# A two-layer hybrid decoder trunk: one product of the first MLP matrix takes an earlier place among seven, and the transfers that build weight sums leave the mixer's last stages

## The chip, the cores and the metric

The kernel runs on one core of one Trainium2 chip. The metric is device time of one execution in microseconds (us), as the median of the runs; smaller is better. The engines are PE (TensorE, matrix products), DVE (VectorE), ACT (ScalarE), POOL (GpSimd) and SP (SyncE, which here only issues transfers). ACT and POOL issue transfers as well, each on a DMA queue of its own.

## The reference

Two layers, each a mixer and an MLP, on 512 tokens of width 1024, all in float32. The mixer's sliding-window attention and its mLSTM are as long as the rest together in code; what the change touches is the end of the mixer and the MLP.

```python
def hybrid_layer(x, ...):
    h = rmsnorm(x, norm_mix)
    z = h @ w_in                      # q,k,v | q,k,v,o of the mLSTM | its gates | branch gates
    ...
    att = sliding_window_attention(q_a, k_a, v_a, att_sinks)
    hm = mlstm_chunkwise(q_m, k_m, v_m, i_pre, f_pre)
    ...
    mixed = sigmoid(g_a) * (att @ w_att_branch) + sigmoid(g_m) * (hm @ w_m_branch)
    x = x + mixed @ w_out
    u = relu(rmsnorm(x, norm_ffn) @ w_ff1)
    return x + (u * u) @ w_ff2        # w_ff1: 1024 x 4096, w_ff2: 4096 x 1024
```

## The kernel before

**Precision.** Every weight and activation is split into a high part `wh` (ACT, a copy that rounds to fp32r) and a low part `wl` (DVE, the difference), and each product is three matmuls, high by high, high by low and low by high (`mm3`). So each weight tile passes through a DMA issued by SP, one ACT instruction and one DVE instruction before PE can use it. In the mixer that is a chunk of 128 x 512 (`chunk`, L192 and L193); in the MLP a block of 128 x 1024 (`w_split`, L915 and L916).

**The mixer** runs one long list of PE work (`weave`, L866) in which a chunk's twelve matmuls have width 1.0: queries, keys and values of attention; then mLSTM queries and keys, branch gates 0 and 1, mLSTM values, the attention branch (`a_steps`, two halves), gate 2, the output gate, gate 3. Attention, mLSTM and head work hang between these as side entries that have a place on the same scale. After it stand the mLSTM branch (the loop with `ev_m`, two halves `g` of the model width, `w_m_branch`) and the output projection (the loop with `ev_x`, `w_out`). `ev_m` takes a finished product out of PSUM with two DVE instructions (L873, L874) and splits it.

**The MLP** runs in four parts. Nearly every 2 x 2 block product is done with seven products and not eight: the plain blocks (0,0), (1,1), (1,0) of a weight matrix are products 1, 3 and 2, and sums of blocks, named A, B, D and C, are products 5, 6, 7 and 4. A is (0,0) + (0,1), D is (0,1) + (1,1), B is (0,0) + D, C is (1,0) + B. `first(part, i, u)` gives the seven products of the first matrix (`w_ff1`) for half `i` of a part, one `Slot` each; a slot is 24 matmuls of 128 x 256. `second(part, u)` gives the seven of the second matrix (`w_ff2`), 48 matmuls of 128 x 512 each in two runs. The slots of `second` of a part and of `first` of the next part are dealt into one list: after each slot of `second` come 2, 2, 2, 2, 3, 3 and 0 slots of `first`, taken in the order of the list that `first` returns.

**PSUM of the first matrix.** Products 1, 6 and 7 add up in bank `a`, 5 and 3 in bank `b`; `a` and `b` are the halves of one two-bank tile `mm`. Products 2 and 4 have a bank of their own, `c` and `d`, from a pool of two called `aux`. Between products of `mm` intermediate values are taken out: `copy` (L1109, ACT) after products 1, 5, 6 and 7, `finish` (L1113 on DVE, then two ACT instructions) after 3, 7, 2 and 4. All of them were recorded before the next product's matmuls, so the next product in `mm` waits for them.

**Weight sums.** A, B, C and D of both matrices are made in DRAM by transfers alone. `plan_sums` puts 79 jobs in a list, in the order in which they are needed: a copy of one half of a block (`Sums.copy`, issued by ACT behind the last weight split, L400, 512 KB), or an add of another onto it (`Sums.add`: POOL copies two numbers of the last weight split into `mark`, L403, and so waits for that split, then issues an accumulating transfer, L405, 512 KB). Each `beat` takes the next job. `beats(...)` places them: 26 in the mixer's long list, at every 2.5 from 2.5 to 40 and then every 2.0 from 42 to 60, 2 in the mLSTM branch, 8 in the output projection, 4 in the MLP's opening, and one after every second run of a slot.

**Order.** The code's order is where work is recorded; a list scheduler in the framework then orders each engine's instructions from it, from priorities (weight loads, splits and evacuations are high) and from its own estimate of durations. On each engine the queue is then fixed and runs in order.

## Time and profile before

| what | value |
|---|---|
| median of 3 runs (lowest to highest) | 1337.94 us (1337.82 to 1338.47) |
| the profiled execution: its own time | 1338.42 us |
| the profiled execution: span from first to last instruction | 1336.7 us |
| DVE, ACT, POOL busy | 72%, 57%, 17% of the span |
| DMA, mean | 177 GB/s |

The page's table of 40 slices shows where the DMA engines are full (each digit is a share in tenths of 33.4 us):

```profile
DMA  5545555689347988975326355565991589889843
```

A layer is half of the row. The 5s and 4s at its start are the mixer; the rise at the ninth and tenth digit is the mLSTM branch, the output projection and the MLP's opening; then come the four MLP parts, thinning out as the sums run out.

A row of the timeline has start, length, engine, line, operation, tile written and tiles read, shape, count, and in brackets the idle time before it with what ended it. A row of waits has the sum of idle time, how many waits, the longest. A row of windows has, for a stretch, each engine's busy time with its count, then the granted clock of PE, the busy share of the DMA engines and GB/s.

### The profile page before, as it was taken

Reading aid. Unit: us, or ns where it says so; the run is one execution under the profiler, and the core shown is the slowest. Engines: PE = TensorE matmul, PEld = TensorE weight load, DVE = VectorE, ACT = ScalarE, POOL = GpSimd, SP = SyncE. Lnnn points to the kernel's source line nnn. Section 1 sums busy time; section 2 is a strip of 40 time slices with the busy share of each in tenths; the row PEclk is TensorE's granted clock in tenths of the full one; section 3 lists DMA queues with packets and bytes.
Section 4 is the critical chain, followed back from the end, with each engine's and each line's share of the span. In section 5 each row is a group of like instructions: output and inputs, shape, how many; then the busy total and the mean of one; then the engine's idle time right before and its main releaser. Section 6 shows DMA issues by size and latency. Waiting matters only on the chain. (4 is left out here: it accounts for less than half of the span.)

```text
span 1336.7 us, 19393 instructions
## 1 busy us (share of the span) xinstructions
PE 1299.9 (97%) x6966; PEld 1101.6 (82%) x6966; DVE 957.3 (72%) x1493; ACT 763.1 (57%) x1367; POOL 225.3 (17%) x371
## 2 busy tenths in 40 slices
PE   8999999989999999999999999999899999999998
PEld 6877788878889889899878777888788898898986
DVE  4689764476568797978847887645746678979786
ACT  5468765544356555666544787554534565555663
POOL 4422410013001200220014134100110011002100
PEclk9999999999999999999999999999999999999999
DMA  5545555689347988975326355565991589889843
GB/s 150 155 128 126 108 135 157 199 237 217 98 140 217 281 214 280 220 208 173 103 80 182 110 136 110 137 191 166 242 247 50 156 228 274 230 258 223 228 153 126
DMA packets 154176, 236.36 MB, mean 177 GB/s; under 512 B 11608, under 2 KB 67008, under 8 KB 154080
## 3 DMA queue, kind: packets, MB, share of 16 engines
q1 hardware_dynamic: 111776, 154.76, 37.1%
q0 software_dynamic: 21056, 39.98, 17.8%
q10 hardware_dynamic: 21248, 40.38, 9.6%
q8 instruction: 55, 0.90, 0.3%
q14 instruction: 41, 0.34, 0.1%
HBM read 232.99 MB, written 81.79 MB: 235 GB/s over the span
## 5 line engine op out<-in xcount | busy, mean ns | idle before, releaser
L47 PE MATMUL mm<-i,wh 128*128 128x512 f32 (+1 forms) x1280 | 353.8, 362 | 1.6 <-ACT kvi L463 1.6
L916 DVE TENSOR_TENSOR wl<-raw,wh 128x1024 fp32r<-128x1024 f32 x212 | 257.1, 1220 | 73.4 <-ACT wh L915 73.1
L915 ACT ACTIVATE wh<-raw 128x1024 fp32r<-128x1024 f32 x212 | 222.4, 1053 | 151.6 <-PE mm L47 109.3
L47 PEld LDWEIGHTS mm<-i,wh 128*128 128x128 f32 x1280 | 224.9, 189 | 34.4 <-ACT kvi L463 2.4
L193 DVE TENSOR_TENSOR wl<-w,wh 128x512 fp32r<-128x512 f32 (+1 forms) x208 | 143.2, 690 | 133.3 <-ACT wh L192 132.3
L47 PE MATMUL mm<-i,wl 128*128 128x512 f32 (+1 forms) x640 | 229.7, 359 | 0.0
L192 ACT ACTIVATE wh<-w 128x512 fp32r<-128x512 f32 (+1 forms) x208 | 127.0, 612 | 163.0 <-PE mm L47 119.5
L403 POOL COPY mark<-wh 1x2 f32<-1x2 f32 x76 | 64.0, 843 | 713.0 <-ACT wh L915 481.4
L47 PE MATMUL mm<-wl,uh 128*128 128x512 f32 x448 | 175.0, 391 | 0.0
L47 PE MATMUL mm<-wh,uh 128*128 128x512 f32 x448 | 175.0, 391 | 0.0
L47 PE MATMUL mm<-wh,ul 128*128 128x512 f32 x448 | 174.6, 390 | 0.0
L47 PE MATMUL mm<-wh,i 128*128 128x512 f32 (+1 forms) x512 | 150.6, 371 | 0.4 <-ACT wh L192 0.4
L47 PEld LDWEIGHTS mm<-i,wl 128*128 128x128 f32 x640 | 120.9, 189 | 17.7
L47 PE MATMUL mm<-hs,wh 128*128 128x256 f32 x576 | 107.4, 287 | 5.5 <-ACT u L1109 5.5
L47 PEld LDWEIGHTS mm<-wh,i 128*128 128x128 f32 x512 | 92.3, 189 | 15.9 <-ACT wh L192 0.8
L47 PEld LDWEIGHTS mm<-hs,wh 128*128 128x128 f32 x576 | 90.0, 191 | 15.5 <-ACT u L1109 14.6
L47 PEld LDWEIGHTS mm<-wh,ul 128*128 128x128 f32 x448 | 84.2, 188 | 16.8
L47 PEld LDWEIGHTS mm<-wh,uh 128*128 128x128 f32 x448 | 84.3, 188 | 16.3
L47 PEld LDWEIGHTS mm<-wl,uh 128*128 128x128 f32 x448 | 84.3, 188 | 16.2 <-DVE wl L916 0.3
L47 PE MATMUL mm<-wl,i 128*128 128x512 f32 (+1 forms) x256 | 94.3, 368 | 0.0
L957 DVE SCALAR_TENSOR_TENSOR x<-mm,ninv,x 128x512 f32<-128x512 f32 x112 | 79.8, 745 | 16.2 <-PE mm L47 15.6
L47 PE MATMUL mm<-wh,a 128*128 128x512 f32 x256 | 82.9, 398 | 5.2 <-DVE a L873 5.2
(243 smaller groups left out, 2140.3 us busy)
## 6 DMA issues: line engine op xcount, KB each, us to landing
raw<-in_w_ff_dram SPq DMA_DIRECT2D x112, 512.0 KB, 6.0
sum<-in_w_ff_dram ACTq DMA_DIRECT2D x76, 512.0 KB, 4.6
raw<-sum SPq DMA_DIRECT2D x76, 512.0 KB, 5.2
w<-in_w_in_dram SPq DMA_DIRECT2D x128, 256.0 KB, 3.0
sum<-in_w_ff_dram POOLq DMA_DIRECT2D x44, 512.0 KB, 8.2
sum<-sum POOLq DMA_DIRECT2D x32, 512.0 KB, 7.5
w<-in_w_out_dram SPq DMA_DIRECT2D x32, 256.0 KB, 5.7
w<-in_w_att_branch_dram SPq DMA_DIRECT2D x16, 256.0 KB, 2.9
```

What stands on the lines that cost most here:

```text
L47: return nc.tensor.matmul(*args, **kw)
L192: last_wh[:] = sc.activation(wh[:, :off], raw[:, :off], AF.Copy), wh
L193: ve.tensor_tensor(wl[:, :off], raw[:, :off], f32(wh[:, :off]), op=ALU.subtract)
L403: m = gp.tensor_copy(mark, f32(last_wh[1][0:1, 0:2]))
L915: last_wh[:] = sc.activation(hi, r, AF.Copy), hi[:, 0, :]
L916: ve.tensor_tensor(lo, r, f32(hi), op=ALU.subtract)
L957: ve.scalar_tensor_tensor(xh[:, i, :], ps[:, i, :], norm.inv[:, 0 if sign > 0 else 1, b:b + 1], xh[:, i, :], op0=ALU.mult, op1=ALU.add)
```

## The change

Two edits. In `first`, product 2 (bank `c`) moves from sixth to third place of the seven, behind product 5 and ahead of product 6; nothing of it is altered. And the beats of the mixer are placed anew: 32 in the long list (every 2.0 from 2 to 40, then every 1.8 from 42 to 61.8), 1 in the mLSTM branch instead of 2, and 2 in the output projection instead of 8. So 35 jobs and not 36 are taken by the end of a mixer, and each later job comes one beat later. No instruction is added or taken out; the counts of rows on ACT, POOL, SP are the same.

```diff
         plan_sums(l)
-        side += beats(*(2.5 * n for n in range(1, 17)), *(42 + 2.0 * n for n in range(10)))
+        side += beats(*(2.0 * n for n in range(1, 21)), *(42 + 1.8 * n for n in range(12)))
@@ the mLSTM branch
             weave(feat_steps(hmT, lambda k, g=g: [w_m_branch[l, k * P:(k + 1) * P, 512 * g:512 * g + 512]], ev_m),
-                  beats(2.0))
+                  beats(2.0) if g == 0 else [])
@@ the output projection
-                  (norm.steps(0, 1.5, 0.5) if j else []) + beats(1.0, 3.0, 5.0, 7.0))
+                  (norm.steps(0, 1.5, 0.5) if j else []) + beats(5.0))
@@ first()
             return [slot(1, "a", True, (copy, 0, 0)), slot(5, "b", True, (copy, 1, 1)),
-                    slot(6, "a", False, (copy, 0, 1)), slot(3, "b", False, (finish, 0, 1)),
-                    slot(7, "a", False, (finish, 1, 1), (copy, 1, 0)),
-                    slot(2, "c", True, (finish, 0, 0)), slot(4, "d", True, (finish, 1, 0))]
+                    slot(2, "c", True, (finish, 0, 0)), slot(6, "a", False, (copy, 0, 1)),
+                    slot(3, "b", False, (finish, 0, 1)), slot(7, "a", False, (finish, 1, 1), (copy, 1, 0)),
+                    slot(4, "d", True, (finish, 1, 0))]
```

What this does to the engines' queues is shown at two places, both of layer 0.

The first is POOL from the end of the mLSTM to the MLP's opening. In the queue before, the adds into sum 627 (second matrix, part 0, D) and sums 620 and 619 (first matrix, part 2, D and A) wait for these splits: 3007 and 3107 are the second and sixth chunk of `w_m_branch`, 3189, 3228, 3266 and 3304 the first, third, fifth and seventh chunk of `w_out`.

```order
L799 AFFINE_SELECT t_2552<-t_2552 128x128
L403 COPY mark<-wh_3007 1x2
L405 DMA sum_627<-in_w_ff_dram 256x512
L403 COPY mark<-wh_3107 1x2
L405 DMA sum_627<-in_w_ff_dram 256x512
L403 COPY mark<-wh_3189 1x2
L405 DMA sum_620<-in_w_ff_dram 256x512
L403 COPY mark<-wh_3228 1x2
L405 DMA sum_620<-in_w_ff_dram 256x512
L403 COPY mark<-wh_3266 1x2
L405 DMA sum_619<-in_w_ff_dram 256x512
```

In the queue now the same adds wait for chunks of the output gate (2704, 2742) and of gate 3 (2797, 2845, 2874, 2921), all ahead of the mLSTM branch. Of the adds into sum 621 (B) that follow, one waits for the second chunk of `w_m_branch` (3019), the other for the fifth of `w_out` (3272):

```order
L799 AFFINE_SELECT t_2556<-t_2556 128x128
L403 COPY mark<-wh_2704 1x2
L405 DMA sum_627<-in_w_ff_dram 256x512
L403 COPY mark<-wh_2742 1x2
L405 DMA sum_627<-in_w_ff_dram 256x512
L403 COPY mark<-wh_2797 1x2
...
L403 COPY mark<-wh_2921 1x2
L405 DMA sum_619<-in_w_ff_dram 256x512
L403 COPY mark<-wh_3019 1x2
L405 DMA sum_621<-sum_620 256x512
L403 COPY mark<-wh_3272 1x2
L405 DMA sum_621<-sum_620 256x512
```

Between the second chunk of `w_m_branch` and the fifth of `w_out` POOL issued three adds and now issues none. Two ACT copies that were hoisted from the MLP's opening to the start of the output projection are there in both queues, and so are the five first loads of MLP weights.

The second place is ACT around product 1 of part 1 (`mm_4752` before, `mm_4750` now). L907 is the split of a left-hand sum for the second matrix, L915 a weight split, L1109 the `copy` that product 5 waits for. Before:

```order
L907 ACTIVATE uh_4785<-s_3735 128x1024
L915 ACTIVATE wh_4705<-raw_4581 128x1024
L915 ACTIVATE wh_4725<-raw_4618 128x1024
L907 ACTIVATE uh_4890<-s_3735 128x1024
L915 ACTIVATE wh_4748<-raw_4746 128x1024
L915 ACTIVATE wh_4780<-raw_4778 128x1024
L1109 ACTIVATE u_3733<-mm_4752 128x2x256
```

Now:

```order
L907 ACTIVATE uh_4783<-s_3734 128x1024
L915 ACTIVATE wh_4724<-raw_4616 128x1024
L400 DMA sum_629<-in_w_ff_dram 256x512
L915 ACTIVATE wh_4746<-raw_4744 128x1024
L915 ACTIVATE wh_4778<-raw_4776 128x1024
L1109 ACTIVATE u_3732<-mm_4750 128x2x256
L907 ACTIVATE uh_4892<-s_3734 128x1024
```

The second L907 stood ahead of two weight splits and the copy, and now stands behind the copy. On PE seven matmuls of the second matrix lie between products 1 and 5 there, before and now.

## The prediction

> **What bounds the kernel now.** I read the page's first part, then what PE waited for, then each of those waits in the timeline.

> ```profile
> span 1336.7 us, 19393 instructions
> PE 1299.9 (97%) x6966; PEld 1101.6 (82%) x6966; DVE 957.3 (72%) x1493; ACT 763.1 (57%) x1367; POOL 225.3 (17%) x371
> ```
> ```profile
> PE mm L47 <- DVE a L873: 7.0, 5, 2.8
> PE mm L47 <- ACT u L1109: 5.5, 7, 1.0
> ...
> PE aux L51 <- DVE t L644: 3.5, 4, 1.5
> PE aux L51 <- DVE t L662: 2.6, 2, 1.3
> PE mm L47 <- ACT kvi L463: 1.6, 2, 1.3
> ```

> PE is the bound: 97% busy, 36.8 us idle. The change leaves its 6966 matmuls alone, so it can only win idle time, and what follows from idle time. The largest named sums are 7.0 us for L873 (the evacuation of the mLSTM branch), which the moved transfers touch, and 5.5 us for L1109 (`copy` between products), which the moved product touches. The sum is made against the profiled execution's own 1338.4 us (span and 1.7 us around it); the median of the runs lies 0.5 us below it, taken off at the end.

> **The change, part by part: the transfers taken from the branch and the output projection.** The five waits for L873 in PE's timeline, three of layer 0 and two of layer 1:

> ```profile
> 287.96 0.74 PE L47 MATMUL mm<-a,wh 128*128 128x512 f32 x2 [0.99 <-DVE a L873]
> 297.29 0.47 PE L47 MATMUL mm<-wh,a 128*128 128x512 f32 x1 [1.74 <-DVE a L873]
> 299.59 0.50 PE L47 MATMUL mm<-wh,a 128*128 128x512 f32 x1 [0.70 <-DVE a L873]
> ```
> ```profile
> 949.60 0.73 PE L47 MATMUL mm<-a,wh 128*128 128x512 f32 x2 [0.76 <-DVE a L873]
> 959.94 0.51 PE L47 MATMUL mm<-wh,a 128*128 128x512 f32 x1 [2.79 <-DVE a L873]
> ```

> Idle: 3.43 and 3.55 us. What held DVE is seen on ACT and POOL (timeline, layer 0) and in the DMA share (windows):

> ```profile
> 285.95 0.63 ACT L192 ACTIVATE wh<-w 128x512 fp32r<-128x512 f32 x1 [2.33 <-DMA w<-in_w_m_branch_dram]
> 294.58 0.63 ACT L192 ACTIVATE wh<-w 128x512 fp32r<-128x512 f32 x1 [3.94 <-DMA w<-in_w_out_dram]
> ```
> ```profile
> 296.46 0.68 DVE L873 TENSOR_TENSOR a<-a,mm 128x512 f32<-128x512 f32 x1
> ```
> ```profile
> 279.11 0.58 POOL L405 DMA_DIRECT2D sum<-in_w_ff_dram  x1
> 290.90 0.74 POOL L405 DMA_DIRECT2D sum<-in_w_ff_dram  x1
> ```
> ```profile
> 280.00:285.00 5.00, 5.00 (x24) 4.14 (x23) 3.17 (x4) 2.85 (x4) 0.00 (x0) 1.00 1.01 283
> 285.00:290.00 5.00, 4.01 (x18) 2.97 (x17) 4.47 (x8) 1.66 (x3) 0.00 (x0) 1.00 1.06 307
> 290.00:295.00 5.00, 5.00 (x24) 4.13 (x23) 1.51 (x3) 1.06 (x3) 1.39 (x2) 1.00 1.07 382
> ```

> The DMA engines are full for 15 us (shares 1.01 to 1.07). ACT sits idle 3.94 us for a `w_out` chunk; its low part on DVE (L193) stands ahead of the L873 at 296.46, the one PE waits for. Queue by queue, the cost of a transfer:

> ```profile
> q1 hardware_dynamic: 111776, 154.76, 37.1%
> q0 software_dynamic: 21056, 39.98, 17.8%
> q10 hardware_dynamic: 21248, 40.38, 9.6%
> ```

> q0 carries the 76 adds: 17.8% of 1336.7 us over 76 is 3.13 us of all 16 engines for one. q10 carries the 76 copies: 1.7 us. q1 carries SP's loads: 3.2 us per MB, so 0.84 us for a chunk of 256 KB. The add issued at 279.11 goes away; in a full stretch the chunk that lands last comes earlier by its 3.13 us, and by some of the add at 290.90. So the split moves from 294.58 to about 291.4, and L873 from 296.46 to 293.3. PE came there at 295.55 (297.29 less 1.74): the waits of 1.74 and 0.70 are covered. In layer 1 PE would have needed 2.79 us and gets 3.1: covered, by little. The first waits (0.99, 0.76) hang on the chunk of `w_m_branch` split at 285.95; the add was half done then, so I give it 1.5 us, of which DVE's queue ahead of L873 hands on about 0.6. Idle won: 1.74 + 0.70 + 2.79 + 2 x 0.6 = 6.4 us. Bounds: 1.2 (only the first waits move) to 7.0.

> The long wait costs more than itself:

> ```profile
> 960.00:964.00 4.00, 4.00 (x11) 2.95 (x12) 4.00 (x8) 1.15 (x2) 0.53 (x1) 0.57 0.75 143
> 964.00:968.00 4.00, 4.00 (x20) 3.30 (x19) 3.91 (x7) 1.82 (x4) 1.53 (x2) 1.00 0.89 225
> ```

> After 2.79 us of idleness the granted clock is 0.57 for 4 us, and 11 matmuls run where 20 do next: 9 of 20, or 1.7 us, are lost. After 1.74 us in layer 0 nothing of the kind is seen. So this part gives 6.4 + 1.7 = **8.1 us**. [...]

> **The moved product.** The four rows of PE that stand for its waits, then ACT around the third:

> ```profile
> 399.33 0.50 PE L47 MATMUL mm<-hs,wh 128*128 128x256 f32 x2 [1.05 <-ACT u L1109]
> 446.15 0.50 PE L47 MATMUL mm<-hs,wh 128*128 128x256 f32 x2 [0.29 <-ACT u L1109]
> 481.32 0.50 PE L47 MATMUL mm<-hs,wh 128*128 128x256 f32 x2 [0.72 <-ACT u L1109]
> 1143.87 0.51 PE L47 MATMUL mm<-hs,wh 128*128 128x256 f32 x2 [0.73 <-ACT u L1109]
> ```
> ```profile
> 477.83 1.06 ACT L907 ACTIVATE uh<-s 128x1024 fp32r<-128x1024 f32 x1 [2.90 <-DVE s L932]
> 478.79 1.99 ACT L915 ACTIVATE wh<-raw 128x1024 fp32r<-128x1024 f32 x2
> 480.69 0.57 ACT L1109 ACTIVATE u<-mm 128x512 f32<-128x512 f32 x1
> ```

> Six of the seven waits are product 5 behind product 1 (399.33, 481.32 and four like them), not product 6 behind 5; one (446.15, 0.29 us) is product 6 behind 5, and only that one is what the new place takes away by itself: 24 matmuls of product 2 now lie between. The others turn on ACT. At 481.32 the copy waits for an L907, which waited 2.90 us for DVE, and two splits. In the new queue that L907 stands behind the copy; the first split can run in the 2.90 us and the second starts when product 1 ends (about 478.6), so the copy comes near 479.6 and ends by 480.2, when PE is through its seven filler matmuls (480.4): 0.72 and its twin 0.73 go. In part 2 of both layers a load is late as well:

> ```profile
> 1222.61 1.06 ACT L915 ACTIVATE wh<-raw 128x1024 fp32r<-128x1024 f32 x1 [0.46 <-DMA raw<-in_w_ff_dram]
> ```

> That split stands ahead of the copy in the new queue too, so these two waits (5.5 less the rows above and their twins: about 1.7 us) may stay; I give them 0.3. In part 0 (399.33 and its twin, 2.1 us) three matmuls of product 2 join the filler, and they need a low part from DVE that is hardly earlier than the copy: nothing. What becomes tight is product 7 behind 3, with some 1.8 us of filler where 2.3 or more lay; what it waits for is one DVE instruction, and no row of PE's waits names L1113: nothing. Sum 0.29 + 0.72 + 0.73 + 0.3 = **2.0 us**, bounds 0 and 4.5.

> **The denser beats in the long list.** They cost ACT's and POOL's queues one issue each, earlier than before, and the DMA engines an add per 2.0 and not 2.5. One row of ACT's new order wins something:

> ```profile
> 48.91 0.62 ACT L192 ACTIVATE wh<-w 128x512 fp32r<-128x512 f32 x1
> 49.44 1.22 ACT L463 ACTIVATE kvi<-mm,ncol 128x264 f32<-128x264 f32 x3
> ```

> The second L463, for which PE waits, stood behind this split and now stands ahead of it: 0.5 us in layer 0, the whole 0.26 us of layer 1 (1.6 less 1.3): **0.7 us**. Elsewhere in attention the scheduler swaps neighbours; L644 and L662 (6.1 us of PE's waits) may gain or lose. No row shows the new order, so I bound it by -3 and +3 us and take 0, the middle. Loads stay covered by this:

> ```profile
> 135.00:170.00 35.00, 32.86 (x157) 25.70 (x156) 25.67 (x63) 25.11 (x73) 14.84 (x25) 1.00 0.57 120
> 320.00:340.00 20.00, 20.00 (x97) 16.45 (x96) 11.06 (x16) 8.26 (x17) 3.06 (x6) 1.00 1.07 287
> ```

> With adds at every 2.5 the DMA share is 0.57; at every 2.0 it is at most 0.57 x 1.25 = 0.71. At 1.07, late in the output projection, PE did not lose a moment. If that cover fails, the price is the last rival's.

> ```profile
> DMA to landing us min/median/max: 4.9/7.9/10.4
> ```

> That is POOL's line of the adds (L405): one lands at most 10.4 us after its issue. The sums come one beat (2.0 us or so) later in the MLP and are issued tens of us ahead of their first reader: nothing.

> **Sum:** 8.1 + 2.0 + 0.7 = 10.8 us; 1338.4 - 10.8 = 1327.6, and less 0.5 for the median **1327.1 us**.

> **The rivals.**
> - *The output projection stays late.* Five loads of 512 KB (1.7 us each) and two ACT copies (1.7 each) remain between 276 and 294, and the shares near 1.05 say that a queue was behind them. If the chunk does not move, only 1.2 of 8.1 us come: 1327.1 + 6.9 = 1334.0. Against: an add costs nearly twice a load.
> - *The change doesn't do what it says in the MLP.* The waits are behind product 1, which did not move. If the copy is no earlier, 0.29 us is won: 1328.8.
> - *Attention's order helps* by the 3 us, and part 2's waits go: 1327.1 - 3 - 1.4 = 1322.7, or lower.
> - *Attention gives the gain back* in small waits (0.5 us each for some twenty reordered places): about 1337.
> - *Slower: a weight chunk in attention's stretch comes as late as the `w_out` chunk did.* Place: adds at the densest beats, first matrix part 1. Price: 2.79 + 1.7 = 4.5 us a time; two in each layer give 18, so 1327.1 + 18 = 1345. It decides from where a chunk lands later than the three raw buffers reach, 3 x 2.7 = 8 us (a chunk's twelve matmuls, 24 of which take 5 us in the windows). For it: adds beside selects on POOL and splits on ACT. Against: share 0.71. [...]

> **How the numbers follow.** Forecast 0.50; output projection late 0.17; no gain in the MLP beyond 0.29 us 0.10; attention helps 0.08; gives back 0.07; slower 0.08. The likeliest is 1327.1. The range goes from 1319.5 (attention helps, its bound and the MLP's 4.5 together) to 1335.0 (the output projection late, 1 us more lost). What a measurement can tell from no change is 0.2%, 2.7 us, so under 1335.3 is faster: 0.50 + 0.10 + 0.08 + 0.15 = 0.83; within 0.09; slower 0.08.

> **What would show it.** Right: no wait for L873 over 1 us near 297 and 958, PE's granted clock 1.00 throughout there, DMA share between 285 and 295 below 1; waits for L1109 at 2 to 4 us in all instead of 5.5; L463 near 0.8. Wrong: ACT still idle 3 us or more for `w_out`; a wait of PE for L192 in attention; L644, L662 and L694 together over 10 us.

## The result and the profile after

| comparison | before, median | changed, median | ratio, 95% interval | saved |
|---|---|---|---|---|
| first | 1338.2 us (4 runs) | 1330.95 us (4 runs) | 0.9938, 0.9918 to 0.9958 | 8.3 us, 5.6 to 11.0 |
| second, beside e8 and e9 | 1341.59 us (17 runs) | 1330.87 us (6 runs) | 0.9927, 0.9909 to 0.9946 | 9.8 us, 7.2 to 12.2 |

The saved time is the ratio's distance from 1 times the median of before. The first lines of the page, and what PE waited for, in the first profile of the changed kernel:

```profile
span 1329.7 us, 19386 instructions
PE 1298.8 (98%) x6966; PEld 1103.2 (83%) x6966; DVE 952.8 (72%) x1493; ACT 766.7 (58%) x1367; POOL 232.2 (17%) x371
```
```profile
PE mm L47 <- DVE a L873: 4.6, 4, 2.6
PE aux L51 <- DVE t L644: 3.6, 6, 1.5
PE aux L47 <- DVE t L694: 2.0, 2, 1.0
PE aux L47 <- DVE wl L916: 1.5, 2, 0.8
...
PE aux L51 <- DVE t L662: 1.4, 2, 0.7
PE aux L47 <- ACT kT L599: 1.3, 2, 0.7
...
PE mm L47 <- ACT kvi L463: 0.2, 1, 0.2
```

The wait for the copies, L1109 (5.5 us before), is gone from this profile (0.5 us in the second); the wait for L873 has only fallen from 7.0 to 4.6 us, and its worst case is nearly what it was in this profile (2.79 us before; in the second profile of each kernel, 2.83 and 1.91 us):

```profile
295.98 0.47 PE L47 MATMUL mm<-wh,a 128*128 128x512 f32 x1 [0.89 <-DVE a L873]
```
```profile
955.89 0.47 PE L47 MATMUL mm<-wh,a 128*128 128x512 f32 x1 [2.65 <-DVE a L873]
```

Both kernels run the same 6966 matmuls, and in the same stages, so the Nth matmul of one trace can be set against the Nth of the other at the borders of stages. The table has the length of each stretch in the profile of before (from the start of one matmul to the start of another), and by how much it is longer (+) or shorter (-) in the profiles of the change and of six experiments (e1 to e9, explained below). This is the table that the rest goes by.

| stretch, matmuls | before, us | change | e1 product | e2 beats | e11 | e4 | e8 | e9 |
|---|---|---|---|---|---|---|---|---|
| 0-300, projections to kvi and on | 59.27 | -1.24 | -1.71 | -0.90 | -1.01 | -0.33 | -1.32 | -1.83 |
| 300-1292, attention to the branch, layer 0 | 207.66 | +1.27 | -0.07 | +0.78 | -0.09 | +0.79 | -0.05 | +2.79 |
| 1292-1804, branch, output projection, MLP's opening | 117.05 | -1.58 | +0.82 | -0.04 | -1.17 | -3.21 | -3.04 | -3.44 |
| 1804-3504, the rest of the MLP, layer 0 | 282.45 | -3.69 | -2.05 | -1.49 | -0.61 | -3.65 | +1.33 | -4.19 |
| 3504-3552, the turn to layer 1 | 11.74 | +1.60 | +1.57 | 0.00 | +1.56 | -0.01 | +1.56 | +1.57 |
| 3552-3800, projections, layer 1 | 46.92 | -0.60 | +0.02 | +0.49 | -0.29 | -0.22 | -0.09 | -0.57 |
| 3800-4774, attention to the branch, layer 1 | 203.72 | +0.80 | +0.09 | +0.71 | -0.06 | +1.07 | -0.01 | +0.52 |
| 4774-5286, branch, output projection, MLP's opening | 118.37 | -0.54 | -0.05 | -1.39 | -3.54 | -5.66 | -5.63 | -5.59 |
| 5286-6965, the rest of the MLP, layer 1 | 278.90 | -3.13 | +2.09 | -0.53 | +0.25 | -3.13 | +1.01 | -3.69 |
| sum | 1326.08 | -7.11 | +0.71 | -2.38 | -4.96 | -14.35 | -6.24 | -14.43 |

It is one execution each. A second profile of before differs from the first by at most 0.75 us in the first seven stretches and by 1.0 us in the last two, and by 2.7 us in the sum; e1's and e2's profiled executions were slower than the median of their runs (1339.3 against 1338.0 us, 1336.2 against 1332.3 us). For what a kernel is worth the ratios count, for where it comes from the table.

In the change 6.8 us come from the two MLPs, 2.1 us from the two branches and output projections, 1.8 us from the projections; attention gives 2.1 us back, and the turn 1.6 us, for a reason of its own (the last section).

### The profile page after: what moved, and what is told of

Read it like the earlier page. It is cut to its first block, busy times and chain, and to the rows that moved or that the text cites. A ratio compares the mean times of both kernels' runs of the same rounds, so it can differ in the third digit from the quotient of the medians.

```text
span 1329.7 us, 19386 instructions
## 1 busy us (share of the span) xinstructions
PE 1298.8 (98%) x6966; PEld 1103.2 (83%) x6966; DVE 952.8 (72%) x1493; ACT 766.7 (58%) x1367; POOL 232.2 (17%) x371
## 3 DMA queue, kind: packets, MB, share of 16 engines
q1 hardware_dynamic: 111776, 154.76, 36.7%
q0 software_dynamic: 21056, 39.98, 18.4%
q10 hardware_dynamic: 21248, 40.38, 9.8%
## 4 chain that ended last, share of the span: by engine, by line
PE 82%; DVE 10%; DMA 3%; ACT 2%; issue 2%; POOL 0%; ACTq 0%; DVEq 0%; SPq 0%; POOLq 0%
PE mm L47 70%; PE aux L47 9%; PE aux L51 2%; DVE wl L916 2%; DVE wl L193 1%; DMA w<-in_w_out_dram 1%; DMA w<-in_w_in_dram 1%; DMA raw<-in_w_ff_dram 1%; ACT wh L915 1%; DVE x L957 1%; DVE ul L908 1%; ACT wh L192 0%; ACT t L657 0%; DVE a L723 0%; DVE t L644 0%
## 5 line engine op out<-in xcount | busy, mean ns | idle before, releaser
L47 PE MATMUL mm<-i,wh 128*128 128x512 f32 (+1 forms) x1280 | 354.4, 362 | 0.6 <-ACT t L841 0.4
L916 DVE TENSOR_TENSOR wl<-raw,wh 128x1024 fp32r<-128x1024 f32 x212 | 256.6, 1219 | 73.3 <-ACT wh L915 73.3
L915 ACT ACTIVATE wh<-raw 128x1024 fp32r<-128x1024 f32 x212 | 223.0, 1055 | 146.3 <-PE mm L47 122.0
L47 PEld LDWEIGHTS mm<-i,wh 128*128 128x128 f32 x1280 | 224.4, 189 | 33.1 <-ACT t L841 1.3
L193 DVE TENSOR_TENSOR wl<-w,wh 128x512 fp32r<-128x512 f32 (+1 forms) x208 | 140.9, 680 | 125.2 <-ACT wh L192 121.6
L47 PE MATMUL mm<-i,wl 128*128 128x512 f32 (+1 forms) x640 | 229.7, 359 | 0.0
L192 ACT ACTIVATE wh<-w 128x512 fp32r<-128x512 f32 (+1 forms) x208 | 127.0, 611 | 157.2 <-PE mm L47 91.4
L403 POOL COPY mark<-wh 1x2 f32<-1x2 f32 x76 | 67.7, 891 | 751.0 <-ACT wh L915 510.6
L47 PE MATMUL mm<-wh,ul 128*128 128x512 f32 x448 | 174.9, 391 | 0.5
L47 PE MATMUL mm<-wh,uh 128*128 128x512 f32 x448 | 175.1, 391 | 0.0
L47 PE MATMUL mm<-wl,uh 128*128 128x512 f32 x448 | 174.8, 390 | 0.0
L47 PE MATMUL mm<-wh,i 128*128 128x512 f32 (+1 forms) x512 | 149.8, 371 | 0.4 <-ACT wh L192 0.4
L47 PEld LDWEIGHTS mm<-i,wl 128*128 128x128 f32 x640 | 120.9, 189 | 17.8
L47 PEld LDWEIGHTS mm<-wh,i 128*128 128x128 f32 x512 | 92.7, 190 | 15.9 <-ACT wh L192 0.8
L47 PE MATMUL mm<-hs,wh 128*128 128x256 f32 x576 | 105.4, 283 | 0.0
L47 PEld LDWEIGHTS mm<-wh,ul 128*128 128x128 f32 x448 | 84.1, 188 | 19.7 <-DVE ul L908 2.2
L47 PEld LDWEIGHTS mm<-wl,uh 128*128 128x128 f32 x448 | 84.3, 188 | 16.1
L47 PEld LDWEIGHTS mm<-wh,uh 128*128 128x128 f32 x448 | 84.3, 188 | 16.0
L47 PE MATMUL mm<-wl,i 128*128 128x512 f32 (+1 forms) x256 | 95.0, 371 | 0.0
L47 PEld LDWEIGHTS mm<-hs,wh 128*128 128x128 f32 x576 | 90.9, 192 | 2.7 <-ACT u L1109 1.3
L47 PE MATMUL mm<-wh,a 128*128 128x512 f32 x256 | 83.1, 398 | 4.3 <-DVE a L873 4.2
```

The source lines that it names most:

```text
L47: return nc.tensor.matmul(*args, **kw)
L192: last_wh[:] = sc.activation(wh[:, :off], raw[:, :off], AF.Copy), wh
L193: ve.tensor_tensor(wl[:, :off], raw[:, :off], f32(wh[:, :off]), op=ALU.subtract)
L403: m = gp.tensor_copy(mark, f32(last_wh[1][0:1, 0:2]))
L915: last_wh[:] = sc.activation(hi, r, AF.Copy), hi[:, 0, :]
L916: ve.tensor_tensor(lo, r, f32(hi), op=ALU.subtract)
```

## The experiments

**e1 and e2: each half of the change alone.** e1 is the kernel before with

```diff
-                    slot(6, "a", False, (copy, 0, 1)), slot(3, "b", False, (finish, 0, 1)),
-                    slot(7, "a", False, (finish, 1, 1), (copy, 1, 0)),
-                    slot(2, "c", True, (finish, 0, 0)), slot(4, "d", True, (finish, 1, 0))]
+                    slot(2, "c", True, (finish, 0, 0)), slot(6, "a", False, (copy, 0, 1)),
+                    slot(3, "b", False, (finish, 0, 1)), slot(7, "a", False, (finish, 1, 1), (copy, 1, 0)),
+                    slot(4, "d", True, (finish, 1, 0))]
```

and e2 the kernel before with the three lines of beats alone.

> Only the moved product (order 1,5,2,6,3,7,4); all transfers as before. Theory A (read from the two traces, weight loads included): the waits of TensorE's weight loads for the copy L1109 (14.6 us, 24 times before; 1.3 us after) carry the gain, 4.5 us in layer 0's MLP and 4.0 us in layer 1's; expected about 8 us faster than before, 1330 us, with L1109's weight-load waits under 2 us and the waits for L873 as before, about 7 us. Rival B (the prediction): this part is worth 2.0 us, 1336 us, and the transfers the rest. If both parts are needed together, neither this run nor the beats alone comes near the whole change.

> Only the moved transfers (denser long list, one beat in the branch, two in the output projection); products as before. Theory A: 1.4 us from the wait for kvi, about 2 us from the waits for L873, some of it given back in attention (up to 1 us) and at the layer's sigmoid L841 (0.7 us): 1 to 3 us faster, 1335 to 1337 us, L1109's weight-load waits still near 14.6 us. Rival B (the prediction): 8.8 us faster, 1329 us.

Measured, against 24 runs of before (median 1340.79 us): e1 1337.97 us, ratio 0.9978 (0.9957 to 0.9998), 3.0 us saved; e2 1332.32 us, ratio 0.9936 (0.9910 to 0.9962), 8.6 us saved. So my theory A fell as a statement on the parts alone, and B's numbers (2.0 and 8.8) lie inside the two intervals. The profile of e1, its waits:

```profile
PE mm L47 <- DVE a L873: 6.1, 4, 3.1
...
PE mm L47 <- ACT u L1109: 3.1, 2, 1.6
...
PE aux L47 <- DVE wl L916: 1.5, 2, 0.8
...
PE mm L47 <- DVE ul L908: 1.3, 2, 0.6
```

The two waits for L1109 are in layer 1's MLP, in the stretches at 1144 and 1225 us. The second on ACT's timeline:

```profile
1223.16 1.06 ACT L915 ACTIVATE wh<-raw 128x1024 fp32r<-128x1024 f32 x1 [3.19 <-DMA raw<-sum]
1224.13 0.58 ACT L1109 ACTIVATE u<-mm 128x512 f32<-128x512 f32 x1
```

The copy stands behind a split whose load, of a sum, came 3.19 us late. With the new beats, in the change, no such wait is left. The product's gain in the MLPs is 6.8 us with the beats beside it, less the 2.0 us that e2's beats win there without it, so 4.8 us; alone it is 0.0 us in this profile (-2.05 and +2.09) and 3.0 us by the runs. The runs can't settle the 4.8: what the change saves beyond e2 is -0.3 us by the first comparison and 1.2 us by the second, each give or take some 4 us.

**e11 and e4: the two copies.** Two copies of ACT, emitted in the MLP's opening, are issued in the middle of the branch, since all that holds them is the last split emitted ahead of them, an L915 that runs there. e4 is the changed kernel, e11 the kernel before, with

```diff
+        kept = list(last_wh)
         for h in range(2):
             for f in plain:
                 f.load(h)
+        last_wh[:] = kept
```

which holds the copies until the last `w_out` chunk is split. It moves two adds of the opening as well (in layer 0 of e4 they are issued at 331.8 and 332.5 us, in the changed kernel at 307.2 and 308.5); in all four kernels these adds are issued behind the waits for L873, so they don't bear on them.

> The changed kernel, with the two copies on ACT's queue (issued at 282.7 and 283.3, and at 940.9 and 941.5) held until the last w_out chunk is split; nothing else moves. Theory C: the two copies (544 packets each way, a queue of their own) hold the w_out chunk in the full stretch of the DMA engines: the chunk then lands 3 us earlier against TensorE's arrival, the waits for L873 (4.6 us) fall under 1 us and the halved clock after 956 us goes: 4 to 6 us faster than the changed kernel, 1325 to 1327 us. Rival D: the 512 KB prefetches of the MLP ahead of the chunk in SP's own queue hold it: waits for L873 stay at 3 us or more, and the time within 1 us of the changed kernel's.

> The kernel before, with only the copies held that ACT issues at 282.6 and 283.1 (and at 944.2 and 944.8): they go behind the last w_out chunk's split; the four adds of the branch and the output projection stay. Theory C: the copies hold the w_out chunk, the adds hardly do: the waits for L873 fall from 7.0 to under 3 us and the clock stays up there: 4 to 6 us faster than before. Rival (the prediction's term): the adds hold it, 3.13 us each: waits for L873 of 5 us or more stay, 0 to 2 us faster. If both are needed: waits of 3 to 5 us.

e4: 1324.63 us, ratio to before 0.9872 (0.9845 to 0.9898), 17.2 us saved and 6.3 us under the changed kernel's median. e11: 1334.72 us, ratio 0.9956 (0.9942 to 0.9969), 5.9 us saved, with all adds of the branch and the output projection where they were. The second `w_out` chunk, for which ACT and then L873 wait, landed this long after its issue:

| kernel | adds in the stretch | copies in the stretch | layer 0 | layer 1 | waits for L873 |
|---|---|---|---|---|---|
| before | yes | yes | 8.4 us | 9.4 us | 7.0 us |
| change | no | yes | 6.9 us | 8.6 us | 4.6 us |
| e11 | yes | no | 6.9 us | 6.7 us | 3.4 us |
| e4 | no | no | 4.6 us | 4.3 us | 0.9 us |

The waits of e11 and e4:

```profile
PE mm L47 <- DVE a L873: 3.4, 5, 0.9
```
```profile
PE mm L47 <- DVE a L873: 0.9, 1, 0.9
```

e4's waits fall under the 1 us that theory C named; e11's 3.4 us is the third case of its expectation, both kinds are needed. Either kind of transfer alone holds the chunk; taken from the kernel before, the copies hold it more (2.1 us on the mean of the layers against 1.1 us for the adds). In the two branch rows of the table together the adds alone are worth 2.1 us, the copies alone 4.7 us, both 8.9 us; the halved clock behind the longest wait is gone in the last two figures, and not in the first (e4's mean granted clock is 1.000; e11's, 0.998, leaves room for one halved stretch, and that one is the +1.56 us of the turn).

**e5: the prefetches.** The changed kernel, with the MLP's first weight loads behind the eighth `w_out` chunk on SP's queue:

```diff
-                    nc.sync.dma_start(raw[:, off:off + n], s)
+                    last_load.append(nc.sync.dma_start(raw[:, off:off + n], s))
...
+        with tc.issue_after(last_load[-9].ins):
-        for h in range(2):
+            for h in range(2):
```

> The changed kernel, with the MLP's eight first weight loads (L948) held on SP's queue behind the eighth w_out chunk; the copies stay. Theory D: these loads stand ahead of the w_out chunks in SP's queue: without them the chunks are issued and land 5 us or more ahead of TensorE, the waits for L873 go to under 0.5 us, and no clock is halved after the output projection's start: 4 to 6 us faster than the changed kernel, 1325 to 1327 us. Rival C: the copies alone fill the stretch: a wait for L873 of 1 us or more stays in each layer. A third way: the MLP's first weights come late instead, with a wait near 341 and 1000 us for L915 or L916: no gain, or slower by the wait.

1344.42 us, ratio 1.0020 (1.0006 to 1.0035): 0.2% slower than before, and 13.5 us above the changed kernel's median. The wait for L873 is gone, and two worse ones have come at the MLP's opening (line numbers are one higher in this kernel):

```profile
PE aux L51 <- DVE i L208: 12.4, 3, 6.7
...
PE mm L47 <- DVE x L886: 5.0, 2, 2.7
```

What they wait for is seen on ACT:

```profile
329.57 0.63 ACT L192 ACTIVATE wh<-w 128x512 fp32r<-128x512 f32 x1 [9.47 <-DMA w<-in_w_out_dram]
```

Theory D is right that these loads hold the first chunks: no wait for L873 is left. But the same jam has moved to the later `w_out` chunks, which now meet the held loads, two copies and two adds and land up to 13.3 us after their issue. Moving loads within the stage did not pay here; the copies are the transfers that can leave it.

**Both kernels again.**

> The kernel before, a second profiled execution. Theory E: the halved clock comes in windows of 3.41 us that start at the clock's own moment, so the same idle time halves the clock in one execution and not in the next; then this profile has another set of halved stretches than the one at 960.24 us, each with a loss of 1.5 to 1.7 us at the layer's turn (672 us) or behind an L873 wait, and the waits themselves are the same within 0.5 us. Rival F: waits and halved stretches are the same in every execution, and the spread of the times has another cause (transfers that land at other times).

> The changed kernel, on the chip of the other runs of this call. Theory E: waits as in the first profile within 0.5 us each (L873 4.6 us in all), with other halved stretches. If the product (3 us alone) and the transfers (8.6 us alone) add up: 11 us under before. If they overlap: 8 us, as in the first comparison.

The changed kernel's second comparison stands in the table at the top: 9.8 us, between "they overlap" and "they add up", both inside its interval. Its waits for L873 are 4.7 us (4.6 in the first profile), those of before 7.2 us (7.0). The sums repeat, but the single waits do not keep within the 0.5 us of theory E: the first of layer 0 is 2.19 us in the second profile of before (0.99 in the first), the long one of layer 1 in the changed kernel 1.91 us (2.65). Nor is the set of halved stretches another: the changed kernel has them at the same two places (669.23 and 955.95 us), before at the same one, twice as long (6.83 us from 959.73). Rival F's premise, that waits are the same in every execution, fails too. What decides between executions is taken up in the last section.

**e7: second place instead of third.**

```diff
-            return [slot(1, "a", True, (copy, 0, 0)), slot(5, "b", True, (copy, 1, 1)),
-                    slot(2, "c", True, (finish, 0, 0)), slot(6, "a", False, (copy, 0, 1)),
+            return [slot(1, "a", True, (copy, 0, 0)), slot(2, "c", True, (finish, 0, 0)),
+                    slot(5, "b", True, (copy, 1, 1)), slot(6, "a", False, (copy, 0, 1)),
```

> The changed kernel, with product 2 in second place (order 1,2,5,6,3,7,4) instead of third. Theory: product 5 then has product 2 ahead of it and the copy of product 1 is covered, but product 6 stands right behind 5 again and waits for that copy: the MLP's windows lie between those of before and of the change, 1 to 4 us slower than the changed kernel. Rival: any place near the front serves, within 1 us of the changed kernel.

1337.28 us, ratio 0.9977 (0.9961 to 0.9992): 6.4 us above the changed kernel's medians, more than the 1 to 4 us expected. The place matters, but not for the reason expected: there are hardly any waits for L1109 (0.2 us), and instead six for the low part of a weight block:

```profile
PE mm L47 <- DVE wl L916: 5.1, 6, 1.1
```

**e8: the copies held, the long list as before.** e4 with the long list's old beats; so six jobs fewer are done by the end of a mixer than in e4.

```diff
-        side += beats(*(2.0 * n for n in range(1, 21)), *(42 + 1.8 * n for n in range(12)))
+        side += beats(*(2.5 * n for n in range(1, 17)), *(42 + 2.0 * n for n in range(10)))
```

> The kernel with the two copies held (e4), but with the long list's old beats (26 at 2.5 and 2.0): so the branch and the output projection keep few transfers, and attention keeps its old order. Theory: the denser list costs 0.8 us in each layer's attention (windows of e4 against before) and wins 0.3 to 1.2 us at kvi: within 1 us of e4. If the six transfers of each layer that now come later in the MLP are late there: slower than e4 by the wait, 1 to 3 us.

1332.00 us, ratio 0.9929 (0.9912 to 0.9945): 7.4 us above e4. Both halves of the expectation show, the second larger than its 1 to 3 us. Attention is back at before's length (-0.05 and -0.01 us in the table, where e4 has +0.79 and +1.07), so the denser list is what attention pays for. And the sums are late: one part of the MLP (matmuls 2867 to 3124, 6349 to 6606) is 4.2 us longer than in before in layer 0 and 4.0 us in layer 1, a halved clock in each among it (the mean granted clock of the execution is 0.996, e4's 1.000). There ACT waits for a sum's load, and the copy behind it is late for PE:

```profile
586.90 1.06 ACT L915 ACTIVATE wh<-raw 128x1024 fp32r<-128x1024 f32 x1 [5.45 <-DMA raw<-sum]
587.86 0.61 ACT L1115 ACTIVATE u<-u 128x512 f32<-128x512 f32 x1
588.38 0.58 ACT L1109 ACTIVATE u<-mm 128x512 f32<-128x512 f32 x1
```

**e9: the last block in the old order.** e4, with the order of before where `part == 3 and i == 1`.

> The kernel with the two copies held (e4), with the old order of products in the last of the eight blocks of the first matrix (part 3, second half) alone. Theory G: the new order there lets two L916 run ahead of L908 on DVE at the end of the MLP, which costs 0.86 us in layer 0 and 0.90 us in layer 1 (weight-load waits for L908, 2.2 us in all): 1 to 1.8 us faster than e4. Rival: the old order brings the wait for L1109 back in that block, 0.3 to 0.9 us a layer: the same as e4.

1324.12 us, ratio 0.9872 (0.9851 to 0.9893), not to be told from e4. In the profile the end of the MLP is as theory G has it. What DVE does there in the changed kernel, and in the kernel before:

```profile
638.23 0.74 DVE L957 SCALAR_TENSOR_TENSOR x<-mm,ninv,x 128x512 f32<-128x512 f32 x1
638.89 2.35 DVE L916 TENSOR_TENSOR wl<-raw,wh 128x1024 fp32r<-128x1024 f32 x2
641.16 1.21 DVE L908 TENSOR_TENSOR ul<-s,uh 128x1024 fp32r<-128x1024 f32 x1
```
```profile
644.42 1.22 DVE L916 TENSOR_TENSOR wl<-raw,wh 128x1024 fp32r<-128x1024 f32 x1
645.55 1.22 DVE L908 TENSOR_TENSOR ul<-s,uh 128x1024 fp32r<-128x1024 f32 x1
```

With one L916 ahead of L908 and not two, e9 has no weight-load wait for L908 left, and each MLP is 0.5 us shorter than in e4 (-4.19 against -3.65, -3.69 against -3.13). The rival's wait came back as well: the weight-load waits for L1109 are 2.6 us (8 of them) and not 1.3 (4), which takes part of the 0.86 and 0.90 us back. In this execution attention of layer 0 took 2.0 us more than in e4, with PE's matmuls there in the same order, so single executions can differ by as much in one stretch.

**e10: attention's beats as before, the rest crowded behind it.** e9 with `*(2.5 * n for n in range(1, 17)), *(42 + 1.2 * n for n in range(16))`.

> The kernel of the run before (copies held, old product order in the last block), with the long list's first 16 beats as in the kernel before (2.5 apart, to 40) and the other 16 at 1.2 from 42, so that the sums are done as early as in the change. Theory: attention (the stretch to 200 us, and its twin) keeps the old order and loses 0.8 to 1.6 us a layer less, against 0.5 us or so more at kvi: 0.5 to 2.5 us under it, 1322 to 1323.5 us. Rival: 16 transfers in the last stretch before the branch crowd the DMA engines, a wait of 1 us or more for L841, L723 or L873: slower.

1337.79 us, ratio 0.9979 (0.9968 to 0.9990): 13.7 us above e9. Attention to matmul 1180 is back at before's length (-0.09 us), and the stretch behind it, up to the branch, 8.25 us longer in layer 0, a halved clock of 6.83 us (from 254.61) among it (the mean granted clock of the execution is 0.994, e9's 0.998):

```profile
PE mm L47 <- ACT t L841: 6.2, 2, 3.7
...
PE mm L47 <- ACT wh L192: 4.2, 3, 2.3
```

A weight chunk (L192) that comes late for PE is the prediction's slower rival. It came not with a job per 2.0 or 1.8 on the list's scale, but with one per 1.2 in the last stages.

## Why the prediction was right in sum and wrong in its terms

**The sum.** 10.8 us were forecast, 8.3 (5.6 to 11.0) and 9.8 us (7.2 to 12.2) measured; 1327.1 us against 1330.9 us, inside the range. The parts alone, 3.0 us (0.3 to 5.8) for the product and 8.6 us (5.1 to 12.1) for the transfers, agree with 2.0 and 8.1 + 0.7. But the trace says that the right numbers were reached by partly wrong steps: in the first profiles the branch and the output projection give 2.1 us where 8.1 were forecast (6.4 of waits, 1.7 of clock), the two MLPs 6.8 us where 2.0 were, and attention loses 2.1 us where none was counted. That these errors cancel is luck. The range's lower end is mis-added besides: 1327.1 less 3 and less what the MLP's bound of 4.5 has beyond the 2.0 already counted is 1321.6, not 1319.5.

The prediction's own signs show the wrong step. Of the signs of being right, a wait for L873 over 1 us stayed near 958 (2.65 us), the clock was halved there (0.50 from 956.67 to 960.08 us), and the DMA share was 1.02 from 285 to 290 us (0.64 from 290 to 295). Of the signs of being wrong, ACT still sat idle over 3 us for `w_out`, in both layers.

**The chunk: the step that failed.** "... in a full stretch the chunk that lands last comes earlier by its 3.13 us": measured from its issue, it came earlier by 1.5 us in layer 0 and by 0.75 us in layer 1. ACT's split moved from 294.58 to 293.28 where 291.4 was forecast:

```profile
293.28 0.63 ACT L192 ACTIVATE wh<-w 128x512 fp32r<-128x512 f32 x1 [3.09 <-DMA w<-in_w_out_dram]
```
```profile
953.19 0.63 ACT L192 ACTIVATE wh<-w 128x512 fp32r<-128x512 f32 x1 [4.84 <-DMA w<-in_w_out_dram]
```

The waits that were to be covered (1.74, 0.70 and 2.79 us) stayed at 0.89, 0.68 and 2.65 us (1.57, 0.70 and 1.91 us in the second profile), and 2.1 us came of a term of 6.4. 3.13 us is the time that an add's packets take, and it was spent as if the engines had no other queue. With the adds gone the copies, issued at the same point, landed 1.0 to 2.1 us sooner after their issue: they took part of the room. From 283 to 286 us in the kernel before, and from 286 to 289 in the changed one, the queues' packets, MB and shares of the engines:

```profile
q0 software_dynamic: 146, 0.30, 60.2%
q1 hardware_dynamic: 206, 0.35, 40.1%
```
```profile
q10 hardware_dynamic: 367, 0.72, 88.5%
q1 hardware_dynamic: 127, 0.12, 11.7%
```

The loads (q1) had 40% of the engines beside the add, and for these 3 us have 12% beside the copies. That is the extreme and not the rule: in the kernel before, from 288 to 291, 390 packets of the copies (65.4%) passed beside 398 of the loads (38.0%), one for one, and in layer 1 of the changed kernel, from 942 to 949, the loads had 47.0%. One figure doesn't hang on the choice of window: the packets of the same two copies (544 of them, 1.05 MB) took 2.7 us of the 16 engines in both layers of before, and 3.5 and 3.2 us in the changed kernel. That copies and loads hold the chunk beside the adds doesn't rest on these shares but on e4, e11 and e5.

The rival "the output projection stays late" named the five loads and the two copies as what would hold the chunk, at 0.17; its mechanism was the true one in good part, and e4, e11 and e5 show it. Its time, 1334.0, did not come, because the chunk moved by some of its way and other terms gave more than forecast.

**The clock.** 1.7 us were to be won because the halved clock behind the 2.79 us would go. It did not: both profiles of the change have it at the same place (from 956.67 and from 955.95 us). The runs have fewer halved stretches all the same: the mean granted clock is 0.9962 over 71 runs of before and 0.9981 over 10 of the change. One stretch lowers the mean by 3.41 x 0.5 / 1336 = 0.0013, so that is, as an estimate, about 1.5 stretches fewer in an execution, and at the 1.56 to 1.60 us that one cost at the turn some 2 us. The term was about right, as a mean over executions, and not at the place it was put. As far as means of so few runs tell, it comes with the transfers: the mean clock is 0.9983 over e2's 7 runs and 0.9955 over e1's 12.

**The product.** The mechanism holds, and it has the two parts that the prediction gave it. Behind product 5 the 24 matmuls of product 2 cover the copy; and as the slots are dealt out anew, 24 matmuls of the second matrix lie ahead of product 3 where seven lay (part 0). Behind product 1 of parts 1 and 2 product 2 adds nothing: there the copy comes earlier on ACT, with L907 behind it. In part 1 of the changed kernel it starts 1.05 us after the end of product 1's stretch on PE (475.81), where it started 2.16 us after it (478.53) in before:

```profile
476.86 0.58 ACT L1109 ACTIVATE u<-mm 128x512 f32<-128x512 f32 x1
477.70 1.06 ACT L907 ACTIVATE uh<-s 128x1024 fp32r<-128x1024 f32 x1 [0.27 <-DVE s L932]
```

In the profiles the size is 4.8 us and not 2.0, for a reason in the reading. Of PE's waits seven were counted, 5.5 us. The weight loads (PEld) tell more, in the kernel before and then in the changed one:

```profile
PEld mm L47 <- ACT u L1109: 14.6, 24, 1.5
```
```profile
PEld mm L47 <- DVE ul L908: 2.2, 4, 0.6
...
PEld mm L47 <- ACT u L1109: 1.3, 4, 0.3
```

24 times a weight load stood idle for the copy, and only seven times PE ran out of matmuls. The other 17 don't show in its own row, yet each cost it some 0.2 us: at 411.92 a load had waited 0.38 us, its matmul started 0.12 us later than where no load waits (0.34 us behind the one ahead of it, against 0.23 at the 12 such places without a wait), and the next one 0.11 us later (0.22 against 0.11). Added up in this way over the starts of matmuls, the 24 waits cost 10.9 us in before (6.9 of them at the six behind product 1) and 9.3 us in e2, those left in the change 0.7 us. The change's new waits in the MLPs, 1.5 us for L916 and 1.8 us for L908, take 3.3 us of that back: 5.3 us beside e2, near the 4.8 of the table. Term by term: part 0 was to win nothing, and won 0.5 us a layer, with the wait now for product 2's low part, L916, 0.77 us, as forecast; part 2's two waits were to stay and went. The new waits for L908 at the end of the MLP (0.86 and 0.90 us) were not looked for, though the order of DVE's work there had them.

**The denser list.** For kvi 0.7 us were forecast: the wait fell from 1.6 to 0.2 us. Attention was set at 0 between -3 and +3: it lost 2.1 us in the two layers (1.7 us in the second profile), and e8 shows that the denser list is the cause. That sums which come one beat later in the MLP cost nothing held for one beat; six beats cost 8.2 us (e8, its two halved stretches among it). That is the use of the denser list: it pays for the transfers that leave the output projection.

## What to carry to other kernels

Read the waits of the weight loads beside those of the matmuls: loads that were late by a few tenths cost PE time here that its own row of waits did not show (10.9 us, of which 5.5 us showed). A transfer's packet time is what it takes, not what its removal gives (3.13 us against 1.5 and 0.75 us here): ask which queue takes its place in the full stretch, and hold every transfer that isn't due there, those first that an order by the last split has let run ahead (here the two copies, alone worth 4.7 us in the branch rows of the table). And transfers taken from one stretch were paid for in another: too late cost the reader (8.2 us in e8), too dense the stage that took them (8.25 us in layer 0 of e10).

## What the runs showed of the hardware

```profile
666.54:669.95 3.41, 1.57 (x9) 1.06 (x10) 2.26 (x5) 2.22 (x5) 0.00 (x0) 1.00 0.49 154
669.95:673.36 3.41, 3.41 (x12) 2.83 (x11) 3.10 (x5) 3.03 (x7) 0.00 (x0) 0.50 0.55 144
...
953.26:956.67 3.41, 0.78 (x4) 0.68 (x5) 2.81 (x5) 1.60 (x3) 0.00 (x0) 1.00 0.25 80
956.67:960.08 3.41, 3.34 (x9) 2.14 (x8) 3.41 (x7) 1.15 (x2) 0.00 (x0) 0.50 0.31 83
```

and at the borders of the first profile of before, around its wait of 1.74 us and its wait of 2.79 us:

```profile
294.65:298.06 3.41, 1.67 (x8) 1.07 (x8) 2.81 (x5) 1.60 (x3) 1.09 (x2) 1.00 1.06 234
298.06:301.47 3.41, 2.71 (x12) 1.93 (x11) 3.41 (x7) 1.27 (x3) 0.00 (x0) 1.00 0.88 140
956.83:960.24 3.41, 0.62 (x3) 0.30 (x2) 2.34 (x4) 1.78 (x3) 0.78 (x2) 1.00 1.01 210
960.24:963.65 3.41, 3.41 (x9) 2.47 (x8) 3.41 (x7) 1.15 (x2) 0.29 (x1) 0.50 0.74 130
```

Behind the window with PE busy for 1.57 us (46%) the clock is halved, behind the one with 1.67 it is not. With windows cut in this way over the whole span, the first profiles of both kernels have no window at full clock (outside the first 15 us and the last 8) with 1.57 us or less without a halved one behind it, and none with 1.67 or more that has one. The windows read in other profiles agree: 1.50 and 1.50 us in the second profile of the change, 1.26 in that of before and 1.33 in e9 have a halved one behind them, 2.00 and 2.74 in the second profile of before have none. So the sentence in the prediction, "After 2.79 us of idleness", named the wrong quantity: in these rows the halved clock goes with the busy time of a window whose place differs from execution to execution, and not with the length of one wait (it follows the turn's 1.46 us in the change, and not the 1.74 us in before). The turn of the layer has the same waits in the first profiles of both kernels (0.41, 0.22 and 1.45 or 1.46 us), and the longest of them, for L207, is 1.5 us in 12 of the 13 profiles; in both profiles of before they fell across a border (2.15 and 2.59 us busy in the two windows of the first, 2.74 and 2.00 in those of the second) and the clock stayed at 1.00, in the change within one window (1.57 us), which is the +1.60 us of the table. e2 and e4 have 0.00 and -0.01 us there.

**What stays open.** e2's runs save 8.6 us and its profile 2.4. By the mean granted clocks the profiled execution had two halved stretches (0.997), four of the seven runs hardly any (0.999 to 1.000), and the first profile of before only one (at 960.24 us), where its runs have about three (0.9962); as an estimate that accounts for some 4 us, and the rest isn't shown. Why the sums' loads are late in e1's layer 1 isn't shown either. In the 3 us of the changed kernel in which the copies held 88% of the engines, 367 of their packets passed beside 127 of loads, where before 390 passed beside 398; loads were outstanding (one issued at 285.07 landed at 292.51), so why fewer of them passed isn't shown. Nor is it shown by profiles that the runs' 8.6 us for the transfers lie where the prediction put them.
